# A feed-forward pair whose product banks ScalarE fills beforehand, with another order of products and of weight sums

## The chip, the core and the metric

The kernel runs on one core of a Trainium2 chip. Its engines are TensorE (PE in the profile), VectorE (DVE), ScalarE (ACT), GpSimd (POOL) and SyncE (SP), which here issues the loads. The metric is the device time in us of one execution; for the kernel before it is the median of three runs.

## What is computed

Two batches, 512 and 256 tokens, go through the same trunk of two layers. The kernel treats them as T = 768 tokens in two halves of H = 384. A layer is a feed-forward, a token mixer (a gated recurrence in the first layer, windowed attention in the second) and a second feed-forward, each on a normalized input and added to x. The change lies in the four feed-forwards:

```
def swiglu_ffn(x, w1, w2):
    gate, up = jnp.split(x @ w1, 2, axis=-1)
    return (jax.nn.silu(gate) * up) @ w2
...
    x = x + 0.5 * swiglu_ffn(rmsnorm(x, norm_g[li, 0]), ffn_w1[li, 0], ffn_w2[li, 0])
```

The model width is 1024 and the hidden width 2816, which is 22 column blocks of 128.

## The kernel before, in words

**Numbers as pairs.** Every fp32 operand of a matmul is split in a high part (a cast on ScalarE: L208 for weights, L319 for data) and a low part (a subtraction on VectorE: L209, L320). A product step is three matmuls: high by high, high by low, low by high.

**A pair by seven products.** A pair (up_pair) computes for one column block the gate and the up half for both token halves. That is a 2x2 block product, and it is done with seven products p1 to p7 instead of eight, from sums of weight blocks and sums of data blocks. Each product is 12 matmuls of 128x384 on L513 (four blocks of the inner width, three matmuls each). The seven results are joined with additions; one line of the join keeps two products in one bank of PSUM, since TensorE can go on adding into a bank. Before, the order of products (table UP) is p1, p7, p2, p5, p4, p6, p3, and the banks are a (p1 and p2), c (p7 and p4), d (p5 and p3) and b (p6 alone). The join: ScalarE copies a (L530) and c (L533) out between their two products, VectorE does L539 (after p5), L543, L544, L547 and L545 (after p6), L550 and L552 (after p3), and ScalarE the two silu operations (L536 in the bank, L551). The result t of the first token half is given out after p6, that of the second, w, after p3.

**A group.** A feed-forward has 22 blocks. The first two are computed plainly (up_plain), blocks 2 to 19 as pairs in five groups of four blocks (the first group has the two plain blocks and two pairs), and the last two blocks as pairs once more; 20 pairs per feed-forward, 80 in all. Four results (two blocks, two halves) are gathered in mix: four subtractions (L422, L423, L433, L434) form the sums t1 to t4 that the second product needs, each split by a cast L319 and a subtraction L320. After four blocks follows down_quad, which multiplies the group with its rows of the second weight, again in seven products p1, p2, p5, p4, p7, p6, p3, now of 18 matmuls of 128x512 (L577, three token blocks), and adds each to x on VectorE (L599). Data factors: p1 takes b00, p2 b10, p3 b11, p4 t4, p5 t1, p6 t2, p7 t3.

**Weights.** They are staged ahead: raw blocks a11, a12, a21, a22 are loaded by SP's queue (L160 and L194, four raw buffers), two sums are formed by accumulating transfers on GpSimd's queue (into, L147: s3 += a11 for p7, a22 += a21 for p4), and two on VectorE in place (L215: the "second" sum a11 += a21 for p6, behind p5's split; the "fourth" sum a12 += a11 for p3, behind p4's split). Eight buffers hold split weights (WBUFS); a pair's product takes one, so staging runs seven products ahead: when a product ends and its buffer is free, the cast for the product after the next six starts. The low part of p5 is formed on GpSimd (L209 with engine POOL), that of the other six on VectorE.

**What sets the order.** The code is written in one order and a scheduler spreads it; each engine then runs its own list in order. PSUM has eight banks of 512 columns (ps). A reader of a bank must be done before the next product that uses the bank.

## Time and profile before

| what | value |
|---|---|
| median of three runs | 2768.75 us (2768.64 to 2768.89) |
| span of the profiled execution (first to last instruction) | 2767.2 us |
| TensorE busy | 2745.0 us, 99% |
| VectorE busy | 2206.5 us, 80% |
| ScalarE busy | 1386.0 us, 50% |
| GpSimd busy | 453.0 us, 16% |
| granted TensorE clock, mean | 0.999 |

The profile shows one execution. Its span leaves out what lies around the first and the last instruction, so the time of a run is some 1.5 us longer than a span. Times are in us unless marked ns. A row of the timeline has the start, the length, the engine, the line, the operation and its tiles, how many instructions are put together, and in brackets how long the engine stood idle ahead of it and what ended that. Names of tiles there: w are split weights, wr and s raw weights, tA data of 384 columns, big the split data, ps a bank of PSUM, x the residual.

### The profile page before, as it was taken

What the parts mean: (1) busy time and instruction counts of PE and PEld (TensorE: products, weight loads), DVE (VectorE), ACT (ScalarE), POOL (GpSimd) and SP (SyncE); (2) the same over time, 40 slices, a digit from 0 to 9 for tenths busy, and PEclk for the clock granted to TensorE, in tenths of its full rate; (3) what the DMA queues carried; (4) which work ended last, traced back from release to release, by engine and by line L of the source; (5) the groups of instructions that cost most, each with busy time, mean ns of one, the idle gap of its engine ahead of it and who ended that gap; (6) DMA issues with size and microseconds to landing.
All of it is one profiled execution on the core that took longest, in us unless ns stands there. A gap on an engine that the chain in (4) does not pass through costs nothing.

```text
span 2767.2 us, 40933 instructions
## 1 busy us (share of the span) xinstructions
PE 2745.0 (99%) x15117; PEld 2554.8 (92%) x15117; DVE 2206.5 (80%) x3766; ACT 1386.0 (50%) x2589; POOL 453.0 (16%) x491
## 2 busy tenths in 40 slices
PE   8999999999999999999999999999999999999998
PEld 8999999989999889999999999999888889999998
DVE  8788788767887888788878887887847868788877
ACT  7344444634455675444445543444458855444443
POOL 2111121200000101211111121111105611211111
PEclk9999999999999999999999999999999999999999
DMA  6554554851122743655444355544424422655443
GB/s 172 130 125 114 126 140 124 227 161 39 39 62 66 205 119 78 143 134 131 115 117 121 78 145 134 126 119 118 130 73 111 89 69 73 145 134 130 114 118 107
DMA packets 352040, 325.22 MB, mean 118 GB/s; under 512 B 14216, under 2 KB 271200, under 8 KB 351840
## 3 DMA queue, kind: packets, MB, share of 16 engines
q1 hardware_dynamic: 303040, 224.56, 27.7%
q0 software_dynamic: 44496, 84.56, 17.4%
q10 hardware_dynamic: 4304, 13.49, 1.3%
q8 instruction: 118, 1.93, 0.3%
q14 instruction: 82, 0.67, 0.1%
HBM read 225.82 MB, written 15.73 MB: 87 GB/s over the span
## 4 chain that ended last, share of the span: by engine, by line
PE 96%; DVE 2%; ACT 1%; DMA 1%; issue 0%; DVEq 0%; POOL 0%; SPq 0%; ACTq 0%; POOLq 0%
PE ps L513 42%; PE ps L577 21%; PE ps L315 6%; PE ps L316 6%; PE ps L314 6%; PE ps L760 5%; PE ps L823 3%; PE ps L928 1%; PE ps L1414 1%; PE ps L904 1%; PE ps L385 1%; PE ps L1426 0%; PE ps L1376 0%; PE ps L1427 0%; PE ps L1377 0%; PE ps L1181 0%
## 5 line engine op out<-in xcount | busy, mean ns | idle before, releaser
L513 PE MATMUL ps<-big,w 128*128 128x384 f32 x6720 | 1169.3, 334 | 0.0
L513 PEld LDWEIGHTS ps<-big,w 128*128 128x128 f32 x6720 | 1165.9, 188 | 1.7 <-ACT tA L530 0.2
L208 ACT CAST w<-wr 128x512 fp32r<-128x512 f32 x600 | 415.8, 707 | 689.2 <-PE ps L513 274.9
L577 PE MATMUL ps<-w,big 128*128 128x512 f32 x2520 | 575.7, 390 | 0.0
L577 PEld LDWEIGHTS ps<-w,big 128*128 128x128 f32 x2520 | 472.7, 188 | 98.0 <-ACT big L319 0.4
L209 DVE TENSOR_TENSOR w<-wr,w 128x512 fp32r<-128x512 f32 (+1 forms) x520 | 438.0, 846 | 145.9 <-ACT w L208 123.9
L147 POOL DMA_DIRECT2D s<-wr x126 | 109.8, 878 | 1250.3 <-DMA s<-in_ffn_w_dram 432.0
L599 DVE SCALAR_TENSOR_TENSOR x<-ps,x 128x512 f32<-128x512 f32 x468 | 302.4, 686 | 10.1 <-PE ps L316 10.0
L314 PE MATMUL ps<-big,w 128*128 128x384 f32 x640 | 219.6, 345 | 1.2 <-ACT w L175 0.9
L315 PE MATMUL ps<-big,w 128*128 128x384 f32 x640 | 215.7, 337 | 0.7 <-DVE big L320 0.7
L316 PE MATMUL ps<-big,w 128*128 128x384 f32 x640 | 214.6, 335 | 0.0
L319 ACT CAST big<-tA 128x384 fp32r<-128x384 f32 x296 | 148.0, 513 | 115.4 <-DVE tA L545 37.0
L147 POOL DMA_DIRECT2D wr<-wr x109 | 94.9, 871 | 518.3 <-DMA wr<-in_ffn_w_dram 165.9
L760 PE MATMUL ps<-w,big 128*128 128x512 f32 x756 | 177.1, 392 | 0.1
L320 DVE TENSOR_TENSOR big<-tA,big 128x384 fp32r<-128x384 f32 x296 | 168.0, 578 | 6.7 <-ACT big L319 4.7
L209 POOL TENSOR_TENSOR w<-wr,w 128x512 fp32r<-128x512 f32 x80 | 137.4, 1718 | 197.8 <-ACT w L208 195.8
L760 PEld LDWEIGHTS ps<-w,big 128*128 128x128 f32 x756 | 140.6, 188 | 29.1 <-DVE w L320 0.6
L215 DVE TENSOR_TENSOR wr<-wr,wr 128x512 f32<-128x512 f32 (+1 forms) x120 | 123.3, 1027 | 25.9 <-issue 23.6
L314 PE MATMUL ps<-w,big 128*128 128x512 f32 x336 | 134.6, 401 | 0.1
L316 PE MATMUL ps<-w,big 128*128 128x512 f32 x336 | 131.8, 392 | 0.5 <-DVE big L400 0.5
L315 PE MATMUL ps<-w,big 128*128 128x512 f32 x336 | 131.8, 392 | 0.0
L315 PEld LDWEIGHTS ps<-big,w 128*128 128x128 f32 x640 | 120.6, 188 | 2.0 <-DVE big L320 1.7
(214 smaller groups left out, 3504.0 us busy)
## 6 DMA issues: line engine op xcount, KB each, us to landing
wr<-in_ffn_w_dram SPq DMA_DIRECT2D x264, 512.0 KB, 4.0
s<-wr POOLq DMA_DIRECT2D x126, 256.0 KB, 4.8
s<-in_ffn_w_dram SPq DMA_DIRECT2D x120, 256.0 KB, 3.2
wr<-wr POOLq DMA_DIRECT2D x80, 256.0 KB, 3.8
wr<-in_hg_w_in_dram SPq DMA_DIRECT2D x32, 512.0 KB, 3.9
wr<-wr POOLq DMA_DIRECT2D x29, 512.0 KB, 4.6
spill<-x ACTq DMA_DIRECT2D x12, 512.0 KB, 4.0
kept<-big POOLq DMA_DIRECT2D x8, 768.0 KB, 9.7
```

The source lines that it names most:

```text
L147: self.nc.gpsimd.dma_start(out, src, accum_op=ALU.add)
L208: nc.scalar.copy(h, src)
L209: (eng or nc.vector).tensor_sub(l, src, h.bitcast(F32))
L314: nc.tensor.matmul(out, a[0], b[0], start=first, stop=False)
L315: nc.tensor.matmul(out, a[0], b[1], start=False, stop=False)
L316: nc.tensor.matmul(out, a[1], b[0], start=False, stop=last)
L319: self.nc.scalar.copy(hi, src)
L320: self.nc.vector.tensor_sub(lo, src, hi.bitcast(F32))
L513: self.nc.tensor.matmul(ps, a[x], b[y], start=first and k == 0 and i == 0, stop=k == 3 and i == 2, skip_group_check=True,)
L577: nc.tensor.matmul(ps, a[x], w[y], start=name == chain and kp == 0 and q == 0, stop=kp == 1 and q == 2, skip_group_check=True,)
L599: self.nc.vector.scalar_tensor_tensor(x, ps, c, x, ALU.mult, ALU.add)
L760: nc.tensor.matmul(ps, x[:, sl], y, start=fresh and k == 0 and q == 0, stop=k == 3 and q == 2, skip_group_check=True,)
```

## The change

The order of products becomes p1, p5, p6, p2, p7, p3, p4. Banks a (p1, p2) and d (p5, p3) are started by a product as before; banks b and c are filled by ScalarE first. After p1, L549 writes the negative of a into b, and p6 is added into b by TensorE; after p6, L555 copies b into c, and p7 and later p4 are added into c. L556 copies b out as well (v), L552 copies d (w), and L559 writes the silu to SBUF. VectorE keeps L562 (after p7), L565, L567 (after p3) and L571 (after p4). The second half's result is now given out first, after p3, and the first half's after p4, so ffn collects results by index. The first pair of a feed-forward takes for b and c the two banks that the last plain block had.

In the weights of pairs the second sum is formed in a21 (a21 += a11, behind p5's split) and the fourth takes it from there (a12 += a21, behind p2's split); p6 uses a21. GpSimd forms the low part of p4 instead of that of p5. The accumulation a22 += a21 is issued ahead of that into s3. At the end of a feed-forward, where the last two blocks are multiplied with the rest of the second weight, the token blocks 0 to 2 (the first half) now take the first of the two column blocks all three in a row before the second one is begun.

```
-UP = ("p1", "p7", "p2", "p5", "p4", "p6", "p3")
+UP = ("p1", "p5", "p6", "p2", "p7", "p3", "p4")
...
+    def seeded(self):
+        return self.wide.pop(0) if self.wide else self.ps(H)
...
         s3 = []
+        if up:
+            self.into(a21, a22)
         for i, src in enumerate(three):
...
-        self.into(a21, a22)
+        if not up:
+            self.into(a21, a22)
...
-        own = {"p1": [a11], "p2": [a12], "p3": [a12], "p4": [a22], "p5": [a21], "p6": [a11], "p7": s3}
+        own = {"p1": [a11], "p2": [a12], "p3": [a12], "p4": [a22], "p5": [a21], "p6": [a21 if up else a11], "p7": s3}
...
+                "second": lambda: nc.vector.tensor_add(a21, a21, a11),
+                "fourth": lambda: nc.vector.tensor_add(a12, a12, a21),
...
-        behind = {"p5": "second", "p4": "fourth"} if up else {}
+        behind = {"p5": "second", "p2": "fourth"} if up else {}
...
-            split(name, own[name], nc.gpsimd if up and name == "p5" else None)
+            split(name, own[name], nc.gpsimd if up and name == "p4" else None)
...
-        a, b, c, d = (self.ps(H) for _ in range(4))
-        v, w, t = (self.tmp(H) for _ in range(3))
+        a, d = (self.ps(H) for _ in range(2))
+        b, c = (self.seeded() for _ in range(2))
+        t, v, w = (self.tmp(H) for _ in range(3))
         p = lambda name, ps, first, last: self.product(key, name, FACTOR[name], ps, first, last)
         p("p1", a, True, False)
-        nc.scalar.copy(v, a)
+        nc.scalar.activation(b, a, AF.Copy, scale=-1.0)
         self.ahead()
-        p("p7", c, True, False)
-        nc.scalar.copy(w, c)
+        p("p5", d, True, False)
+        nc.scalar.copy(w, d)
+        self.ahead()
+        p("p6", b, False, True)
+        nc.scalar.copy(c, b)
+        nc.scalar.copy(v, b)
         self.ahead()
         p("p2", a, False, True)
-        nc.scalar.activation(a, a, AF.Silu)
+        nc.scalar.activation(t, a, AF.Silu)
         self.ahead()
-        p("p5", d, True, False)
-        nc.vector.tensor_sub(w, w, d)
+        p("p7", c, False, False)
+        nc.vector.tensor_sub(w, c, w)
+        self.ahead()
+        p("p3", d, False, True)
+        nc.vector.tensor_sub(v, d, v)
+        self.last_act = nc.scalar.activation(v, v, AF.Silu).ins
+        nc.vector.tensor_mul(w, v, w)
+        yield 1, w
         self.ahead()
         p("p4", c, False, True)
-        p("p6", b, True, True)
-        nc.vector.tensor_sub(v, v, b)
-        nc.vector.tensor_sub(t, c, v)
-        nc.vector.tensor_mul(t, t, a)
-        yield t
-        nc.vector.tensor_sub(w, w, v)
-        self.ahead()
-        p("p3", d, False, True)
-        nc.vector.tensor_add(v, v, d)
-        self.last_act = nc.scalar.activation(v, v, AF.Silu).ins
-        self.last_dve = nc.vector.tensor_mul(w, v, w).ins
-        yield w
+        self.last_dve = nc.vector.tensor_mul(t, c, t).ins
+        yield 0, t
...
-            for i, k in (((0, 0), (1, 0), (0, 1)), ((1, 1),))[b] if b < 2 else ((b, 0), (b, 1)):
+            for i, k in (((0, 0), (1, 0), (2, 0), (0, 1)), ((1, 1),), ((2, 1),))[b] if b < 3 else ((b, 0), (b, 1)):
```

Lines move: the weight cast is L215 in the changed kernel, its split L216, the sums L224 and L225, the data's cast and split L335 and L336, mix has L438, L439, L449 and L450, the products L531, those of the down quad L596, their addition L618, the accumulating transfer L151. Numbers behind a tile's name tell tiles of one kind apart.

ScalarE's list in the third pair of a group (first feed-forward, fourth group of blocks), from the silu of the pair ahead on; big are the split sums of the gather, wr and s3 raw weights. Before:

```order
L551 ACTIVATE tA_409_2798<-tA_409_2798 128x384
L530 COPY tA_429_2945<-ps_425_2941 128x384
L208 CAST w_432_2961<-s3_403_2772 128x512
L319 CAST big_419_2919<-tA_410_2799 128x384
L533 COPY tA_430_2946<-ps_427_2943 128x384
L208 CAST w_433_2977<-wr_401_2768 128x512
L319 CAST big_421_2927<-tA_392_2663 128x384
L536 ACTIVATE ps_425_2941<-ps_425_2941 128x384
L208 CAST w_434_2993<-wr_402_2770 128x512
L319 CAST big_422_2932<-tA_411_2800 128x384
L319 CAST big_423_2935<-tA_410_2799 128x384
L319 CAST big_424_2938<-tA_393_2664 128x384
```

After, with the new pair's banks ps_423 (a), ps_425 (b), ps_424 (d) and ps_426 (c):

```order
L335 CAST big_417_2905<-tA_407_2785 128x384
L549 ACTIVATE ps_425_2929<-ps_423_2927 128x384
L215 CAST w_430_2947<-wr_399_2756 128x512
L335 CAST big_419_2913<-tA_391_2652 128x384
L552 COPY tA_429_2933<-ps_424_2928 128x384
L335 CAST big_420_2918<-tA_407_2785 128x384
L335 CAST big_421_2921<-tA_409_2787 128x384
L335 CAST big_422_2924<-tA_389_2650 128x384
L215 CAST w_431_2964<-wr_399_2756 128x512
L555 COPY ps_426_2930<-ps_425_2929 128x384
L556 COPY tA_428_2932<-ps_425_2929 128x384
```

The copies of the new pair's second bank, L533 before, stood third from the top of the casts; L555, the copy that fills bank c, now stands behind three casts L335 of the gather and a weight cast.

VectorE's list at the same place, the gather itself (wr are the raw weights in which a sum is formed, tA the pair's results). Before:

```order
L552 TENSOR_TENSOR tA_410_2799<-tA_409_2798,tA_410_2799 128x384
L209 TENSOR_TENSOR w_432_2961<-s3_403_2772,w_432_2961 128x512
L320 TENSOR_TENSOR big_419_2919<-tA_410_2799,big_419_2919 128x384
L422 TENSOR_TENSOR tA_410_2799<-tA_392_2663,tA_410_2799 128x384
L423 TENSOR_TENSOR tA_392_2663<-tA_393_2664,tA_392_2663 128x384
L209 TENSOR_TENSOR w_433_2977<-wr_401_2768,w_433_2977 128x512
L433 TENSOR_TENSOR tA_393_2664<-tA_393_2664,tA_410_2799 128x384
L320 TENSOR_TENSOR big_421_2927<-tA_392_2663,big_421_2927 128x384
L434 TENSOR_TENSOR tA_411_2800<-tA_411_2800,tA_393_2664 128x384
L215 TENSOR_TENSOR wr_401_2768<-wr_401_2768,wr_402_2770 128x512
```

After:

```order
L567 TENSOR_TENSOR tA_409_2787<-tA_408_2786,tA_409_2787 128x384
L571 TENSOR_TENSOR tA_407_2785<-ps_406_2784,tA_407_2785 128x384
L336 TENSOR_TENSOR big_415_2886<-tA_409_2787,big_415_2886 128x384
L216 TENSOR_TENSOR w_418_2908<-wr_398_2754,w_418_2908 128x512
L336 TENSOR_TENSOR big_417_2905<-tA_407_2785,big_417_2905 128x384
L438 TENSOR_TENSOR tA_409_2787<-tA_391_2652,tA_409_2787 128x384
L439 TENSOR_TENSOR tA_391_2652<-tA_389_2650,tA_391_2652 128x384
L216 TENSOR_TENSOR w_430_2947<-wr_399_2756,w_430_2947 128x512
L449 TENSOR_TENSOR tA_389_2650<-tA_389_2650,tA_409_2787 128x384
L336 TENSOR_TENSOR big_419_2913<-tA_391_2652,big_419_2913 128x384
L450 TENSOR_TENSOR tA_407_2785<-tA_407_2785,tA_389_2650 128x384
L224 TENSOR_TENSOR wr_399_2756<-wr_399_2756,wr_398_2754 128x512
```

Before, the chain to the last subtraction L434 began with L552; now it begins with L571, has L567 ahead of it and one more split L336 within, and ends with L450; the sum of raw weights stands behind it in both.

TensorE's list in the down quad of the same group: p2 (factor b10, tile big_416 before, big_417 after) and p5 (factor t1, big_421 before, big_419 after), with the banks of the three token blocks. Before:

```order
L577 MATMUL ps_465_3230<-w_453_3130,big_416_2894 128x512
L577 MATMUL ps_465_3230<-w_454_3131,big_416_2894 128x512
...
L577 MATMUL ps_466_3238<-w_453_3130,big_416_2894 128x512
...
L577 MATMUL ps_467_3246<-w_453_3130,big_416_2894 128x512
...
L577 MATMUL ps_472_3286<-w_455_3177,big_421_2927 128x512
L577 MATMUL ps_472_3286<-w_456_3178,big_421_2927 128x512
```

After:

```order
L596 MATMUL ps_463_3214<-w_451_3116,big_417_2905 128x512
L596 MATMUL ps_463_3214<-w_452_3117,big_417_2905 128x512
...
L596 MATMUL ps_470_3270<-w_453_3146,big_419_2913 128x512
L596 MATMUL ps_470_3270<-w_454_3147,big_419_2913 128x512
...
L596 MATMUL ps_471_3278<-w_453_3146,big_419_2913 128x512
L596 MATMUL ps_471_3278<-w_454_3147,big_419_2913 128x512
L596 MATMUL ps_471_3278<-w_453_3146,big_419_2913 128x512
L596 MATMUL ps_464_3222<-w_451_3116,big_417_2905 128x512
...
L596 MATMUL ps_465_3230<-w_451_3116,big_417_2905 128x512
```

Before, p5 followed all three token blocks of p2; now its first token block and half of its second stand ahead of p2's second.

22 lines of the change are left out of this document (16 added, 6 removed).

## The prediction

> **What bounds the kernel now.** I read the page first: busy time, and the chain that ended last by engine.
>
> ```profile
> span 2767.2 us, 40933 instructions
> PE 2745.0 (99%) x15117; PEld 2554.8 (92%) x15117; DVE 2206.5 (80%) x3766; ACT 1386.0 (50%) x2589; POOL 453.0 (16%) x491
> PE 96%; DVE 2%; ACT 1%; DMA 1%; issue 0%; DVEq 0%; POOL 0%; SPq 0%; ACTq 0%; POOLq 0%
> ```
>
> TensorE is busy for 99% of the span and carries 96% of the chain. The change touches what stands around the products of the pairs (L513) and of the down quads (L577) and takes no matmul away. So the next view is that of line L513 alone: how long TensorE stood before these matmuls, and who waited for them.
>
> ```profile
> L513 PE MATMUL ps<-big,w x6720: 333/334/445, 52.1 to 2742.7; 128*128 128x384 f32 x198
> its engine sat idle before it (us, times) until:
>   ACT tA L530: 0.2, 1
> who waited for it (us, times):
> ...
>   ACT tA L533: 82.9, 76
>   DVE tA L539: 78.6, 59
> ```
>
> In 6720 matmuls TensorE waited once. The readers of the banks wait for TensorE instead: ScalarE's L533 in 76 of 80 pairs, VectorE's L539 in 59. The 21 that are missing there are pairs in which VectorE came late and TensorE still did not wait. The timeline gives the pace, and the chain in order of time the price of that one wait (start, us, what).
>
> ```profile
> 299.80 42.28 PE L513 MATMUL ps<-big,w 128*128 128x384 f32 x243
> 341.92 28.76 PE L577 MATMUL ps<-w,big 128*128 128x512 f32 x126
> 52.23 29.25 PE ps L513 x168
> 457.55 29.14 PE ps L513 x168
> ```
>
> A matmul of 128x384 takes 0.1733 us (243 in 42.28, the last one's 0.33 overlapping), so a product of 12 takes 2.08 and a pair of 84 takes 14.56; one of 128x512 takes 28.76/126 = 0.227 (nearly). Two pairs take 29.14 where nothing waits and took 29.25 at the start of the first feed-forward: that is the wait, 0.11 us. The kernel ends when TensorE has done its work, so an operation taken from VectorE or ScalarE is worth nothing by itself. The question is whether the new order makes TensorE wait.
>
> **The change, part by part.** *The join.* New operations are named by the changed kernel's lines. Per group of instructions the columns are busy us, mean ns | idle before.
>
> ```profile
> L544 DVE TENSOR_TENSOR tA<-ps,tA 128x384 f32<-128x384 f32 x80 | 44.2, 552 | 0.8
> L536 ACT ACTIVATE ps<-ps 128x384 f32<-128x384 f32 x80 | 38.0, 475 | 57.8 <-PE ps L513 57.8
> ```
>
> VectorE had seven operations of this size per pair, of 0.55 us each, and keeps four: 3 x 80 x 0.55 = 132 us less. ScalarE goes from four to six: 2 x 80 x 0.475 = 76 us more, each costed as L536, which reads and writes a bank as the new L549 and L555 do. VectorE is at 80% and ScalarE at 50%, neither carries the chain, so both sums are worth 0 while their work stays ahead of TensorE. TensorE's own work is the same 84 matmuls; a product that adds into a filled bank issues the same matmuls as one that starts a bank, so 0.
>
> What is new is three short links, each with one product of cover: p1, then L549 on ScalarE, then p6; p6, then L555, then p7; p7, then L562 on VectorE, then p4. In an ordinary pair the cover holds. Let S be the start of a pair; the pair below starts at S = 341.92 - 2 x 14.56 = 312.80.
>
> ```profile
> 313.62 0.55 DVE L550 TENSOR_TENSOR tA<-tA,ps 128x384 f32<-128x384 f32 x1
> 314.08 0.69 DVE L209 TENSOR_TENSOR w<-wr,w 128x512 fp32r<-128x512 f32 x1
> 315.08 0.48 ACT L530 COPY tA<-ps 128x384 f32<-128x384 f32 x1 [0.35 <-PE ps L513]
> 315.16 0.56 DVE L552 TENSOR_TENSOR tA<-tA,tA 128x384 f32<-128x384 f32 x1
> 315.45 0.62 ACT L208 CAST w<-s 128x512 fp32r<-128x512 f32 x1
> 315.97 0.52 ACT L319 CAST big<-tA 128x384 fp32r<-128x384 f32 x1
> 316.11 0.69 DVE L209 TENSOR_TENSOR w<-s,w 128x512 fp32r<-128x512 f32 x1 [0.40 <-ACT w L208]
> 319.62 0.62 ACT L208 CAST w<-wr 128x512 fp32r<-128x512 f32 x1
> 319.91 0.55 DVE L434 TENSOR_TENSOR tA<-tA,tA 128x384 f32<-128x384 f32 x1
> 320.49 1.34 ACT L319 CAST big<-tA 128x384 fp32r<-128x384 f32 x3 [0.25 <-DVE tA L434]
> 321.74 0.62 ACT L208 CAST w<-wr 128x512 fp32r<-128x512 f32 x1
> 324.21 0.54 DVE L539 TENSOR_TENSOR tA<-tA,ps 128x384 f32<-128x384 f32 x1
> ```
>
> The copy of the first product starts at 315.08, 0.20 after that product's end at S + 2.08, and takes 0.48. What comes from ScalarE to TensorE takes 0.15 more: at the start of the first feed-forward a copy L530 delayed p2 by the 0.11 found above,
>
> ```profile
> 52.07 6.19 PE L513 MATMUL ps<-big,w 128*128 128x384 f32 x34
> 55.72 0.47 ACT L530 COPY tA<-ps 128x384 f32<-128x384 f32 x1
> ```
>
> and p2 was due at 52.07 + 4.16 = 56.23, so it started at 56.34, 0.15 after that copy's end at 56.19. A link so takes 0.20 + 0.48 + 0.15 = 0.83 of the 2.08 that the product between gives: 1.25 us are spare in each ordinary pair, and the same for L562 with 0.55 instead of 0.48. Cost 0. If the cover were gone, each us of queue beyond 1.25 would be a us of the kernel.
>
> *The pair after a gather.* There the queue is long, and this is where the sum is made. Four groups of each of four feed-forwards have such a pair (the third of the group), and the first pairs of the second to fourth feed-forward follow the gather of the plain columns: 16 + 3 = 19. In the new order ScalarE has the casts of the last three sums of the gather (t4, t3, t2) and one weight cast ahead of L555, and these wait for VectorE's chain that ends in L450 (L434 before). Before, the copy L533 stood ahead of them.
>
> The chain starts earlier now. Its first operation is the last multiply, L571, which can start at S + 0.20, where L552 started at 315.16 = S + 2.36. But L567, ahead of it, can be held by GpSimd's split of p4, which the change puts here. Its cast starts 0.20 after p3's end (S - 2.08), thus at S - 1.88, and ends at S - 1.26.
>
> ```profile
> 305.06 0.61 ACT L208 CAST w<-wr 128x512 fp32r<-128x512 f32 x1
> 305.76 1.29 POOL L209 TENSOR_TENSOR w<-wr,w 128x512 fp32r<-128x512 f32 x1 [1.97 <-ACT w L208]
> 320.13 0.87 POOL L147 DMA_DIRECT2D s<-wr  x1 [6.39 <-DVE big L320]
> 320.38 2.50 DVE L215 TENSOR_TENSOR wr<-wr,wr 128x512 f32<-128x512 f32 x1
> 320.69 1.63 POOL L209 TENSOR_TENSOR w<-wr,w 128x512 fp32r<-128x512 f32 x1
> ```
>
> GpSimd starts 0.09 after its cast (305.06 + 0.61 to 305.76) and takes 1.29 alone: S - 1.17 to S + 0.12. A VectorE operation with both inputs in SBUF that met such a split, L215 at 320.38, ended at 322.88, 0.56 after GpSimd's 322.32 instead of 0.68 after its own start; scaled to L567's 0.55 that is 0.45, so L567 ends at S + 0.57 and L571 starts 0.09 before that (operations start that much before the end shown of the one ahead, 313.62 + 0.55 = 314.17 against the next at 314.08), at S + 0.48. The Trainium skill, page "SBUF — State Buffer", section "Who interferes with whom", says that whichever of the two starts first holds the shared access for its whole instruction and blocks the other fully. By that rule L567 would run whole after GpSimd, 0.10 later than I take; in this case's trace the operation needed less than its own time after GpSimd's end, so the measurement decides.
>
> From the chain's first operation to its last took 320.46 - 315.16 = 5.30 before. The new chain has one more split of a hidden block in it (+0.46, as from 313.62 to 314.08) and loses the idle 0.40 that stood before 316.11: 5.36. L450 ends at S + 5.84. Then 0.03 to the casts (320.46 to 320.49), 1.25 for the three (to 321.74), 0.52 for the weight cast (315.45 to 315.97), 0.48 for L555 and 0.15 to TensorE: S + 8.27. p7 is due after four products, at S + 8.32. So the sum stands 0.05 us inside; with no hold by GpSimd it would stand 0.33 inside. With so little spare, some pairs will fall on the other side of the line, and I take 0.05 us of wait a pair on average: 19 x 0.05 = 0.95 us. Ends: 0 (no better, since there is no wait here to save), and the 0.65 a pair of the first rival.
>
> VectorE's link in that pair: L539 was held to 324.21 by the same backlog, S + 11.41. L562 inherits that place at the worst; with 0.55 and 0.15 it is done at S + 12.11, due for p4 at S + 12.48. Cost 0.
>
> *The down quad.* There the order now starts p5 after 24 matmuls instead of 36.
>
> ```profile
> 342.59 1.22 DVE L209 TENSOR_TENSOR w<-wr,w 128x1024 fp32r<-128x1024 f32 x1
> 344.19 0.55 DVE L552 TENSOR_TENSOR tA<-tA,tA 128x384 f32<-128x384 f32 x1
> 344.66 0.69 DVE L599 SCALAR_TENSOR_TENSOR x<-ps,x 128x512 f32<-128x512 f32 x1
> 348.87 0.56 DVE L320 TENSOR_TENSOR big<-tA,big 128x384 fp32r<-128x384 f32 x1
> ```
>
> Let D = 341.92 be its start. p5's sixth matmul needs the low half of t1, by D + 29 x 0.227 - 0.15 = D + 6.43. Before, that split came 4.68 after L552. Between the same two there are now two accumulations fewer (2 x 0.69), one split more (0.46) and one of 128x1024 (1.22): 4.98. From L571 at D + 0.20 to 0.48 and with its own 0.56 it ends at D + 5.7 to 6.0, at least 0.4 early. Cost 0; if VectorE comes 0.6 later than that, 0.2 a quad, 4 us in 20.
>
> *The weights.* Casts, splits and sums are the same in number; p4's split takes p5's place on GpSimd. The second sum must now follow p5's split and p6's cast follows that sum: they are on the path to L555 only in the gather pair, where the sum is done before the three casts are. Of the accumulating transfers on GpSimd's queue (320.13 is one) none is added. SP's loads of the feed-forwards keep their order. What is staged is 7 products, 14.5 us, ahead, so a split that lands 1 us later costs 0. At the end of a feed-forward the first half's values now come last. They are needed after three adds of six matmuls, 18 x 0.227 = 4.09 after p4; L571 (0.55), w's split (0.56), t's cast (0.52) and split (0.56) behind the 0.20 make 2.39: 0.
>
> *Sum.* The one wait of 0.11 goes, since in the first pair L555 stands ahead of the casts. 0.95 - 0.11 = 0.84 on the profiled span of 2767.2 gives 2768.0; 1.55 lies around that span in the median run (2768.75), so **2769.6 us**. A measurement of this kernel can tell about 0.2%, 5.5 us, from no change.
>
> **The rivals.** *GpSimd in the way, slower.* The split of p4 often does not run alone. At 320.69 it started 0.36 later than its cast allowed (319.62 + 0.62 + 0.09 = 320.33), behind the issue of a transfer at 320.13, and took 1.63. With the longer time alone L567 ends 0.34 later and L555 is 0.29 too late: 19 x 0.29 = 5.5, 2774.3. With the issue ahead too, 0.65 too late: 12.4, 2781.1. With one half of the pairs of each kind, 2777.7. It decides where L450 ends later than S + 5.89. For it: of the two splits quoted one is of the long kind. Against it: at S - 1.9 VectorE has just got its operand from TensorE and meets GpSimd with one such operation, not with a row of them as at 320.38.
>
> *The down quad waits.* t1's low half comes late by 0.2: 2769.6 + 4 = 2773.6. For it: a backlog such as that at 324.21. Against it: 0.4 to 0.7 spare.
>
> *Relief pays, faster.* VectorE loses 132 us, and TensorE's wait for it at the start of a feed-forward (us, times, longest) shrinks.
>
> ```profile
> PE ps L315 <- DVE big L320: 0.7, 2, 0.3
> ```
>
> With the 0.1 above that is at most 0.8: 2767.9. To be faster by over 0.2% it would have to find 5.5 us, which no wait on these lines holds.
>
> **How the numbers follow.** Forecast, 0 to 0.2 us of wait a pair (2768.6 to 2772.5): 0.62. GpSimd in the way: 0.24, of which 0.17 lies above 2774.25. The down quad: 0.07, of which 0.01 above. Relief: 0.07, of which I leave 0.03 for a gain that the waits do not show. So faster 0.03, same 0.79, slower 0.18. The range goes from 2767.0 (relief, less the 0.25 us between the runs of before and as much again for waits too short for the views, and rounded down) to 2778.0, which leaves out 0.10 at the slower rival's upper end and some 0.04 at the other side.
>
> **What would show it.** Right: the products' line again without waits, or with a few of under 0.3 us, all on ScalarE's L555 and in the third pair of a group; VectorE's busy time near 2075, ScalarE's near 1462; L450 ending near S + 5.85. The slower rival: GpSimd's split of p4 at 1.6 us or more and L567 ending behind it in the pair before, with 0.3 to 0.7 us of wait on L555 each time. Wrong altogether: waits of TensorE on L549 or L562 in ordinary pairs, a pace other than 0.173 us for products into filled banks, or a time under 2763.

## The result, and the profile after

| what | before | after |
|---|---|---|
| median of the runs on one chip | 2768.69 us (2768.46 to 2768.89, four runs) | 2807.51 us (2802.03 to 2809.55, four runs) |
| span of the profiled execution | 2767.2 us | 2807.8 us (that run: 2809.55 us) |

The ratio is 1.0137, with an interval of 1.0124 to 1.0151: the kernel became 1.4% slower. The forecast was 2769.6 us, with a range up to 2778.0. It was wrong, in size and in place. Of the executions of all the kernels below one stands apart, one of ten of weights_only with 3904.03 us; the ratio given there is of the other nine.

One statement ahead of the prediction must be corrected first. The accumulating transfer into(out, src) adds src to out, so into(a21, a22) makes **a21 += a22, the operand of p5**, and p4 uses the raw a22. The text says in two places that the transfer is a22 += a21 and makes the operand of p4. The change moves p5 from the fourth place to the second, so the product that comes early is the one whose operand arrives by a transfer.

The page of the changed kernel, busy time and the chain that ended last:

```profile
PE 2760.6 (98%) x15117; PEld 2550.0 (91%) x15117; DVE 2104.8 (75%) x3526; ACT 1440.3 (51%) x2749; POOL 443.8 (16%) x491
PE 70%; DVE 13%; DMA 9%; ACT 4%; issue 3%; POOL 1%; ACTq 0%; DVEq 0%; POOLq 0%; SPq 0%
```

VectorE lost 240 instructions (3766 to 3526) and ScalarE gained 160, as forecast, and VectorE is 102 us less busy (2105, forecast 2075; ScalarE 1440, forecast 1462). TensorE's share of the chain fell from 96% to 70%; VectorE, the transfers and ScalarE came in. The waits of TensorE (what it waited for: us, times, longest):

```profile
PE ps L596 <- DVE x L618: 14.5, 17, 3.1
...
PE ps L531 <- DVE tA L562: 5.5, 4, 1.9
...
PE ps L531 <- ACT ps L555: 0.5, 3, 0.2
```

L596 are the matmuls of the down quads. Before, VectorE's additions to x (L599 then, L618 now) held them once, for 0.3 us. The view of waits has 17 such waits; the distances between the starts of neighbouring matmuls, which also hold what follows a wait, show the short ones too. Counted is what exceeds the usual distance (0.226 us in quads, 0.173 in pairs) by more than 0.06:

| part | before | after | where in a quad of 126 matmuls |
|---|---|---|---|
| quads, up to the 100th matmul | 0.3 us | 15.4 us (14 of 20 quads over 0.2) | from the 19th on, p2's first, into p1's first bank |
| quads, from the 100th on | 0.0 us | 10.0 us (17 of 20) | from the 109th on, p3's first, into p7's first bank |
| pairs | 0.1 us | 7.9 us | 6.6 of it at p4 behind L562, in the pair after each fifth quad; 1.3 at p7 behind L555, in the first pair of the later three feed-forwards |

These make 32.9 of the 40.6 us between the two spans. The other 7.7 lie in smaller distances and outside pairs and quads, and were not followed. The new order of token blocks at a feed-forward's end was not tried alone; edges_old below has it too and is 5.8 us slower in all.

**The 109th matmul.** A bank of p7 is free for p3 when VectorE has added it to x. In the quad that starts at D = 348.00 the chain in order of time runs through VectorE's list from one sum of the second weight (L229) to that addition:

```profile
359.59 1.14 DVE wr L229
...
360.75 4.37 DMA wr<-in_ffn_w_dram
...
365.78 5.82 DMA wr<-wr
...
371.75 0.63 ACT w L215
...
372.41 0.69 DVE w L216
373.10 0.61 DVE x L618
...
373.85 4.33 PE ps L596 x18
```

A raw weight block of the coming pair is loaded (4.37 us) when the sum has freed its buffer, then a22 is added into a21 by a transfer from SBUF to SBUF (issued at 365.78, 5.82 us), then ScalarE casts p5's high part and VectorE forms the low part. Only behind that step stands the addition that frees the bank. VectorE's own rows there, with the idle time in brackets:

```profile
367.77 0.68 DVE L216 TENSOR_TENSOR w<-wr,w 128x512 fp32r<-128x512 f32 x1
372.41 0.69 DVE L216 TENSOR_TENSOR w<-wr,w 128x512 fp32r<-128x512 f32 x1 [3.96 <-ACT w L215]
373.02 0.69 DVE L618 SCALAR_TENSOR_TENSOR x<-ps,x 128x512 f32<-128x512 f32 x1
```

VectorE is idle for 3.96 us, waiting for a weight that TensorE needs only a product (2.08 us) after the quad's end, and the additions of p7 wait behind it in its list. Nothing else holds them: VectorE has been idle since 368.45. TensorE started 1.44 after the step L216; the matmul was due at D + 108 x 0.2266 = D + 24.47, so VectorE must go on, that is start the step it waited for, by D + 23.03. It went on at D + 24.41 here, at D + 23.88 in the median of the 20 quads. The same place before, in the quad that starts at 341.92:

```profile
361.63 0.88 POOL L147 DMA_DIRECT2D wr<-wr  x1 [6.05 <-DVE w L209]
...
363.28 1.88 DVE L599 SCALAR_TENSOR_TENSOR x<-ps,x 128x512 f32<-128x512 f32 x3
...
365.07 0.69 DVE L209 TENSOR_TENSOR w<-wr,w 128x512 fp32r<-128x512 f32 x1
367.90 0.69 DVE L215 TENSOR_TENSOR wr<-wr,wr 128x512 f32<-128x512 f32 x1 [2.14 <-issue]
```

The transfer was issued later, 19.71 us after the quad's start against 17.78 now. VectorE had its idle time here too (2.14 us, and the row names no releaser) and went on at D + 25.98, later than now. But the three additions at 363.28 stood ahead of it, not behind it: p5 was the fourth product, so its steps stood further down the list. So it held nobody.

**The 19th matmul.** The worst case is the first quad of the kernel, D = 80.33:

```profile
79.94 2.00 ACT L215 CAST w<-wr 128x1024 fp32r<-128x1024 f32 x2 [5.10 <-DMA wr<-wr]
81.02 1.23 DVE L216 TENSOR_TENSOR w<-wr,w 128x1024 fp32r<-128x1024 f32 x1 [4.09 <-ACT w L215]
82.16 0.55 DVE L565 TENSOR_TENSOR tA<-ps,tA 128x384 f32<-128x384 f32 x1
...
83.78 0.55 DVE L571 TENSOR_TENSOR tA<-ps,tA 128x384 f32<-128x384 f32 x1
...
86.99 0.69 DVE L618 SCALAR_TENSOR_TENSOR x<-ps,x 128x512 f32<-128x512 f32 x1
```

and TensorE there:

```profile
80.33 4.28 PE L596 MATMUL ps<-w,big 128*128 128x512 f32 x18
87.73 4.44 PE L596 MATMUL ps<-w,big 128*128 128x512 f32 x12 [3.12 <-DVE x L618]
```

Here the late weight is the quad's own p5. ScalarE waits 5.10 us for its accumulating transfer, VectorE 4.09 us for the cast. In VectorE's list this split of 1.23 us stands ahead of the last pair's join (L565, L567, L571), which opens the gather, which stands ahead of the first L618. That one starts at D + 6.66; before it started 2.74 after D in the quad of the prediction's rows (344.66 less 341.92), and it must start by D + 18 x 0.2266 - 0.74 = D + 3.34. The median over the 20 quads went from 2.74 to 3.66. Why the quad's p5 comes later: the last raw block that its transfer needs goes into the buffer that the last pair's a22 leaves, and a22 is now held by p4, the last product, whose low part GpSimd forms. In the fourth quad (D = 348.00):

```profile
333.88 1.63 POOL L216 TENSOR_TENSOR w<-wr,w 128x512 fp32r<-128x512 f32 x1
...
339.75 0.88 POOL L151 DMA_DIRECT2D wr<-wr  x1 [4.25 <-DMA wr<-in_ffn_w_dram]
...
344.37 1.05 ACT L215 CAST w<-wr 128x1024 fp32r<-128x1024 f32 x1 [1.86 <-DMA wr<-wr]
345.45 1.22 DVE L216 TENSOR_TENSOR w<-wr,w 128x1024 fp32r<-128x1024 f32 x1 [0.85 <-ACT w L215]
```

In the median the load of that block starts at D - 12.48, 0.03 after GpSimd's split ends, against D - 14.39 before; the accumulation is issued at D - 8.07 against D - 9.74, and VectorE splits the quad's p5 at D - 2.31 against D - 3.91. It takes both the place and the engine: p5_second below, where GpSimd forms p4's low part but p4 is the fifth product, loses nothing at the 19th, and join_only, where p4 is last but VectorE splits it, 2.6 us.

**The pair after the fifth quad.** L562 frees the way for p4, and VectorE comes late to it, behind six updates of x (L611 and L612) and the weights' steps:

```profile
1493.13 0.68 DVE L611 TENSOR_TENSOR x<-x 128x512 f32<-128x512 f32 x1
...
1501.43 0.55 DVE L562 TENSOR_TENSOR tA<-ps,tA 128x384 f32<-128x384 f32 x1
```

TensorE stands for 1.93 us ahead of p4. It happens once in each of the four feed-forwards, for 0.82 to 1.93 us each.

**The place of the forecast's sum**, the third pair of a group. At S = 318.88:

```profile
324.78 1.34 ACT L335 CAST big<-tA 128x384 fp32r<-128x384 f32 x3 [1.11 <-DVE tA L450]
...
326.55 0.47 ACT L555 COPY ps<-ps 128x384 f32<-128x384 f32 x1
```

The casts start at S + 5.90 (forecast S + 5.87), L555 at S + 7.67 and is done at S + 8.14, 8.12 by the forecast. The step that leads there came as forecast too: GpSimd's split of p4 runs from S - 1.17 to S + 0.11, and L567, held by it, ends at S + 0.52 (forecast S + 0.57). No third pair waits. The one sum that was worked out to the hundredth came out, and it was not where the time went.

### The profile page after: what moved, and what is told of

Read it like the earlier page. It is cut to its first block, busy times and chain, and to the rows that moved or that the text cites. A ratio compares the mean times of both kernels' runs of the same rounds, so it can differ in the third digit from the quotient of the medians.

```text
span 2807.8 us, 40688 instructions
## 1 busy us (share of the span) xinstructions
PE 2760.6 (98%) x15117; PEld 2550.0 (91%) x15117; DVE 2104.8 (75%) x3526; ACT 1440.3 (51%) x2749; POOL 443.8 (16%) x491
## 4 chain that ended last, share of the span: by engine, by line
PE 70%; DVE 13%; DMA 9%; ACT 4%; issue 3%; POOL 1%; ACTq 0%; DVEq 0%; POOLq 0%; SPq 0%
PE ps L531 29%; PE ps L596 12%; PE ps L331 6%; PE ps L332 6%; PE ps L330 6%; PE ps L779 4%; DMA wr<-wr 4%; DVE w L216 3%; PE ps L842 3%; DMA wr<-in_ffn_w_dram 3%; DVE x L618 2%; DVE big L336 2%; ACT w L215 2%; PE ps L947 1%; PE ps L1433 1%
## 5 line engine op out<-in xcount | busy, mean ns | idle before, releaser
L531 PE MATMUL ps<-big,w 128*128 128x384 f32 x6720 | 1171.7, 334 | 6.0 <-DVE tA L562 5.5
L531 PEld LDWEIGHTS ps<-big,w 128*128 128x128 f32 x6720 | 1165.0, 188 | 11.1 <-DVE tA L562 6.8
L215 ACT CAST w<-wr 128x512 fp32r<-128x512 f32 x600 | 414.2, 706 | 617.0 <-PE ps L531 165.6
L216 DVE TENSOR_TENSOR w<-wr,w 128x512 fp32r<-128x512 f32 (+1 forms) x520 | 427.4, 829 | 250.8 <-ACT w L215 240.2
L596 PE MATMUL ps<-w,big 128*128 128x512 f32 x2520 | 587.3, 392 | 15.1 <-DVE x L618 14.5
L596 PEld LDWEIGHTS ps<-w,big 128*128 128x128 f32 x2520 | 470.0, 188 | 127.4 <-DVE x L618 17.1
L618 DVE SCALAR_TENSOR_TENSOR x<-ps,x 128x512 f32<-128x512 f32 x468 | 306.4, 684 | 14.7 <-PE ps L332 13.7
L151 POOL DMA_DIRECT2D s<-wr x126 | 110.7, 886 | 1222.2 <-DVE wr L229 350.2
L335 ACT CAST big<-tA 128x384 fp32r<-128x384 f32 x296 | 146.8, 512 | 133.0 <-DVE tA L438 44.5
L216 POOL TENSOR_TENSOR w<-wr,w 128x512 fp32r<-128x512 f32 x80 | 124.6, 1558 | 397.1 <-ACT w L215 397.1
L336 DVE TENSOR_TENSOR big<-tA,big 128x384 fp32r<-128x384 f32 x296 | 164.1, 566 | 25.8 <-ACT big L335 21.4
L779 PE MATMUL ps<-w,big 128*128 128x512 f32 x756 | 177.2, 392 | 0.1
L151 POOL DMA_DIRECT2D wr<-wr x109 | 95.1, 873 | 403.3 <-DVE x L618 121.6
L330 PE MATMUL ps<-w,big 128*128 128x512 f32 x336 | 134.7, 401 | 1.3 <-ACT big L415 0.7
L331 PE MATMUL ps<-w,big 128*128 128x512 f32 x336 | 131.8, 392 | 0.0
L332 PE MATMUL ps<-w,big 128*128 128x512 f32 x336 | 131.7, 392 | 0.0
L331 PEld LDWEIGHTS ps<-big,w 128*128 128x128 f32 x640 | 120.4, 188 | 2.7 <-DVE big L336 2.6
L330 PEld LDWEIGHTS ps<-big,w 128*128 128x128 f32 x640 | 119.8, 188 | 3.2 <-ACT w L179 1.7
```

The source lines that it names most:

```text
L151: self.nc.gpsimd.dma_start(out, src, accum_op=ALU.add)
L215: nc.scalar.copy(h, src)
L216: (eng or nc.vector).tensor_sub(l, src, h.bitcast(F32))
L330: nc.tensor.matmul(out, a[0], b[0], start=first, stop=False)
L331: nc.tensor.matmul(out, a[0], b[1], start=False, stop=False)
L332: nc.tensor.matmul(out, a[1], b[0], start=False, stop=last)
```

## The experiments

All times are medians beside runs of the kernel before on the same chip. The three numbers in brackets are the excess of the distances between matmuls, as in the table above: quads up to the 100th matmul / from there on / pairs. The kernel before has 0.3 / 0.0 / 0.1, the changed one 15.4 / 10.0 / 7.9.

**Which pairs carry the loss?** Four kernels take the old order, join and sums for some pairs of each feed-forward and the new ones for the rest. With the list set to (4, 8, 12, 16, 20) it is the first pair after each quad (first_old), with (3, 7, 11, 15, 19) the last pair before each (last_old), with both lists edges_old, with (6, 10, 14, 18) the third pair of the groups (third_old).

```
-                self.plan_quad((tag, i), (gate, up), (NC, P), UP)
+                self.plan_quad((tag, i), (gate, up), (NC, P), UPO if i in PLAIN_PAIRS else UP)
...
+        if j in PLAIN_PAIRS:
+            yield from self.up_pair_old(tag, j)
+            return
```

> The first pair behind each down quad (blocks 4, 8, 12, 16, 20) keeps the order, join and weight sums of before; the other 60 pairs are changed. Theory, three places (in the trace of the changed kernel TensorE stands 15.4 us at the 19th matmul of the down quads, where p2 adds into p1's banks behind VectorE's late L618, 10.0 us at the 109th, where p3 adds into p7's banks while VectorE is blocked by the split of the next pair's p5, and 6.6 us on L562 in the pair after the fifth quad): the second and third place go, the first stays: 2807.5 - 16.6 = 2791, waits at the 109th matmul under 1 us in all, at the 19th still about 15. Rival, the new join costs the same in every pair (38.8/80 = 0.49 us): 20 pairs give back 9.7, 2797.8. Forecast's own mechanism (ScalarE's chain in the pair after a gather): nothing, 2807.

Measured: 2792.29 us, ratio 1.0082 (1.0067 to 1.0097), (15.9 / 0.0 / 1.4). As expected: the 109th matmul no longer waits, and the waits in the pairs after the fifth quad are gone too.

> The last pair ahead of each down quad (blocks 3, 7, 11, 15, 19) keeps what was before, the other 60 are changed. Theory of the three places: its second result comes out after p3 and its first after p6 as before, so VectorE's gather is done earlier, L618 follows p1 in time and the 15.4 us at the 19th matmul go; the other two places stay: 2807.5 - 15.4 = 2792. Rival, the same cost in every pair: 2797.8. Forecast's own mechanism: 2807.

Measured: 2844.51 us, ratio 1.0272 (1.0255 to 1.0289), (0.6 / 58.4 / 9.5). The 19th is free, as expected, but the kernel is 37 us slower than the changed one. The waits of TensorE:

```profile
PE ps L635 <- DVE x L657: 41.8, 21, 3.7
```

Nearly all are at the 109th now (L657 is the addition to x here). VectorE goes on at D + 25.64 in the median, against 23.88, because the transfer comes later after D: it is issued at D + 19.24 in the median, against D + 17.97. It is issued at D + 19.2 to 19.5 in the kernels whose last pair ahead of a quad ends with p3 (the kernel before, this one, and edges_old, weights_only, p5_second and p5_second_pool below), and at D + 17.5 to 18.0 where that pair ends with p4; why was not followed. So taking away one place made the other worse, and the sizes of the two can't be added or taken away one by one. It is not that the wait at the 19th had hidden the other. In the changed kernel a longer wait at the 19th moves the transfer and VectorE back by about as much: in the first quad 4.8 us are lost there, VectorE goes on at D + 28.08, and the 109th loses 0.2.

> First and last pair of each group (both sets, 40 pairs) keep what was before. Theory of the three places: both savings add up, 2807.5 - 32 = 2775.5; what is left over 2768.7 is the start of the second to fourth feed-forward (L555, 1.3 us) and some 4 us outside the pairs and quads. Rival, the same cost in every pair: 2807.5 - 19.4 = 2788.

Measured: 2774.64 us, ratio 1.0019 (1.0010 to 1.0028), (0.9 / 0.0 / 1.3). As expected. Half of the pairs have the new join, order and sums, and that costs 5.8 us in all.

> The third pair of the later groups (blocks 6, 10, 14, 18, sixteen pairs: those that follow a gather) keeps what was before. Theory of the three places: these pairs carry no wait, so nothing changes, 2807 (2803 to 2810). Rival, the same cost in every pair: 2807.5 - 7.8 = 2799.7. The forecast's place (L555 behind the casts of the gather): if the loss came from there, it would go almost whole, 2769 to 2775.

Measured: 2808.07 us, ratio 1.0135 (1.0120 to 1.0150), (14.1 / 5.7 / 12.3). As expected: the time of the changed kernel, though the three places share the loss otherwise. The place on which the forecast spent its care carries nothing.

**Is it the transfer, and what else stands in the list?** The kernel a22_dve leaves the accumulating transfer out in pairs. A sum on VectorE takes its place, a22 += a21 behind p5's split, so p5 uses a21 alone and p4 uses a21 + a22; these are other sums than the reference's, and the kernel is read for its waits alone. first_add has the first product of the quad written ahead of the gather, and the gather issued behind the first L618. both_fixes is the two together, with a22_dve's sums.

```
-        if up:
-            self.into(a21, a22)
...
+            if up and name == "p5":
+                pin(nc.vector.tensor_add(a22, a22, a21))
```

```
-                gather(ts, kp)
-            self.down_quad(tag, g, hid)
...
+                    quad = self.down_quad(tag, g, hid)
+                    next(quad)
+                    with self.tc.issue_after(self.first_add):
+                        gather(ts, kp)
+                    for _ in quad:
+                        pass
```

> All pairs are changed, but the sum a22 += a21 is formed by VectorE (behind p5's split) and not by an accumulating transfer, so the cast of p5 waits for the load of the raw weights alone; VectorE gets 80 additions of 0.68 us more. Theory (VectorE is blocked near the end of a down quad by the split of the next pair's p5, whose cast waits for the accumulating transfer into the same raw tile, and the L618 behind it frees p7's banks for p3): the 10.0 us at the 109th matmul go, and the 6.6 us on L562 in the pair after the fifth quad for the most part, since that backlog comes from the same wait; the 15 us at the 19th stay: 2793 (2789 to 2798). Rival, the raw load itself or the mere place of the split ahead of L618 holds VectorE: the waits at the 109th stay, 2807 or more for the added work.

Measured: 2802.82 us, ratio 1.0125 (1.0109 to 1.0140), (24.5 / 0.0 / 4.5). Without the transfer in the coming pair the 109th does not wait, as expected. The 19th grew from 15.4 to 24.5, which was not, and the time lies above the range on record. In this kernel the quad's own p5 is split later still, at D - 1.56 in the median against D - 2.31; why was not followed.

> All pairs are changed; in a group's end p1 of the down quad is written ahead of the gather, and the gather's subtractions are issued behind the first L618. Theory: L618 starts at D + 2.75 as before the change (now a median of 3.66), the waits at the 19th matmul go (at most 3 us stay, in quads where the split ahead waits for a transfer), and TensorE reaches the 109th matmul earlier, in time for the same block of VectorE: as in the run with the old last pairs, whose waits at the 109th rose from 10 to 50 us, 2840 (2830 to 2846). Rival, the loss in that run came from the mixture of old and new pairs itself: 2792.

Measured: 2800.59 us, ratio 1.0118 (1.0103 to 1.0133), (7.6 / 9.9 / 6.8). Neither number came out. The first addition starts at D + 3.16 in the median, and half of the excess at the 19th stays: in those quads the last pair's join itself is late behind p5's split, and the additions wait for it whatever their place. The 109th did not grow as in last_old, with half of the excess at the 19th gone.

> Both edits together, all 80 pairs with the new join: a22 += a21 on VectorE and p1 of the quad ahead of the gather. Theory: neither wait is left, and what remains over 2768.7 is the start of three feed-forwards (1.3 us), some of L562 after the fifth quad and the 4 us outside pairs and quads: 2773 (2770 to 2778). Rival, each place costs by itself and the run with the first add moved stays bad for another reason: over 2790.

Measured: 2796.45 us, ratio 1.0106 (1.0090 to 1.0121), (17.4 / 0.0 / 4.2). Not as expected: the time is the rival's. The same is left at the 19th, L565 behind the quad's own p5, which is late here as in a22_dve (D - 1.64).

> The kernel before with the weight part of the change alone: a21 += a11 behind p5's split, p6 from a21, the fourth sum from a21 behind p4's split, p4's low part on GpSimd, the accumulation into a22 issued first; the order of products and the join are those of before. Theory: p5 is the fourth product there, three L599 stand ahead of its split on VectorE, and no wait of TensorE arises: 2769 (2768 to 2772). Rival, the sums in the other operand are what costs: 2790 to 2810.

The opposite cut: the kernel before, with the new sums and with p4's low part on GpSimd, and the old order and join.

```
+        su = (a21, a11) if up else (a11, a21)
...
-            split(name, own[name], nc.gpsimd if up and name == "p5" else None)
+            split(name, own[name], nc.gpsimd if up and name == "p4" else None)
```

Measured: 2769.85 us, ratio 1.0003 (0.9993 to 1.0013), (0.5 / 0.0 / 2.5). As expected: with p5 in the fourth place neither the sums nor the swap of engines costs anything that can be told.

> All 80 pairs with the new join and the new weight sums; only the sum a21 += a22, p5's operand, is formed by VectorE ahead of p5's cast, in pairs and down quads, instead of by an accumulating transfer on GpSimd's queue (100 additions, 79 us more for VectorE). Theory (all waits come from p5's operand landing late, since p5 now stands second in a pair and the down quad's raw blocks are loaded later: at the 109th matmul VectorE is blocked by the next pair's p5 with L618 behind it, at the 19th by the quad's own p5 ahead of L565 and L571): both waits and most of L562's after the fifth quad go, 2773 (2770 to 2779). Rival, VectorE's order at the quad's start (L618 behind the gather) costs by itself: the waits at the 19th stay, 2785 to 2792. Rival, the join costs in every pair: above 2800.

The changed kernel with a21 += a22 formed by VectorE ahead of p5's cast, in pairs and quads; the sums are the reference's, and no accumulating transfer into a21 is left.

```
-            self.into(a21, a22)
...
+            if name == "p5":
+                pin(nc.vector.tensor_add(a21, a21, a22))
```

Measured: 2793.23 us, ratio 1.0090 (1.0075 to 1.0105), (0.4 / 0.0 / 18.3). In the quads everything is gone: without the transfer neither wait is there. But the time is 20 us above the number on record, since another wait came, in all 16 third pairs:

```profile
PE ps L529 <- DVE tA L560: 13.1, 16, 0.8
```

L560 is L562 of the changed kernel. The forecast gave that link 0.37 us of spare there. The added sum of the coming pair (L235) stands ahead of it in VectorE's list, and VectorE then stands until the cast behind the sum is done:

```profile
323.38 0.68 DVE L235 TENSOR_TENSOR wr<-wr 128x512 f32<-128x512 f32 x1
324.80 0.69 DVE L212 TENSOR_TENSOR w<-wr,w 128x512 fp32r<-128x512 f32 x1 [0.73 <-ACT w L211]
```

**Which part of the change brings p5 to the front of the list?** p5_second is the kernel before with p5 second (order p1, p5, p7, p2, p4, p6, p3), the second sum behind p2, and p4's low part on GpSimd instead of p5's; p5_second_pool the same order with p5's low part left on GpSimd. join_only is the changed kernel with the old sums and with p5's low part on GpSimd, join_p4_pool the same with p4's on GpSimd: one word apart. p5_pool is the changed kernel, new sums too, with p5's on GpSimd.

```
-            split(name, own[name], nc.gpsimd if up and name == "p5" else None)
+            split(name, own[name], nc.gpsimd if up and name == "p4" else None)
```

> The kernel before, with the old join and the old sums, but with p5 moved from the fourth to the second place (p1, p5, p7, p2, p4, p6, p3) and its low part formed by VectorE, p4's by GpSimd; the second sum stays behind the fourth product. Theory: VectorE's list has the split of p5 ahead of the three additions of p7; its operand lands as late as before the change (VectorE went on at D + 25.5), TensorE needs p7's banks at D + 24.5 and gets them 1.44 after VectorE goes on: 2.4 us in each of 20 quads, 2768.7 + 48 = 2817 (2795 to 2825). Rival, the join with filled banks is what costs: 2769.

Measured: 2828.14 us, ratio 1.0212 (1.0197 to 1.0227), (0.0 / 59.2 / 0.4).

```profile
PE ps L577 <- DVE x L599: 40.6, 19, 3.5
```

Slower by 60 us with the old join, and above the range on record. It waits at the 109th alone, in all 20 quads.

> As the run with p5 moved to the second place in the kernel before (2828.1), but p5's low part stays on GpSimd. Order, join and sums are the same as there. Theory (not the place of p5 as such costs, but that a step of p5 that waits for its transfer stands in VectorE's list ahead of the additions that free p7's banks): the three additions stand ahead of everything that waits, 2770 (2768 to 2773). Rival, the earlier demand for p5's operand costs by itself, on whatever engine: 2800 or more.

Measured: 2775.22 us, ratio 1.0026 (1.0016 to 1.0037), (0.0 / 0.0 / 5.4). With p5's split on GpSimd the same order costs 6 us instead of 60, some 2 above the range on record; 4.6 us of its excess lie in the pairs after the fifth quads.

> The changed kernel, but GpSimd forms the low part of p5 as before the change, VectorE that of p4. Theory: the last raw block of a group is free some 0.7 us earlier (VectorE's 0.68 instead of GpSimd's 1.3 or more), the quad's own p5 lands earlier and the waits at the 19th matmul shrink from 15 to under 8; at the 109th the sum L224 now waits for GpSimd's split of p5 behind the landing (0.62 and 1.3 to 1.6 us instead of 0.66), with all three additions behind it: 10 grows to some 35. Together 2824 (2812 to 2832). Rival, the split of p5 on VectorE is itself the trouble, not its operand: the waits at the 109th go, 2790 to 2797.

Measured: 2839.43 us, ratio 1.0257 (1.0242 to 1.0272), (7.2 / 36.0 / 21.5). Worse than the changed kernel, as expected, and by more. With the new sums the second sum a21 += a11 overwrites p5's operand, so VectorE's list has a step that must follow GpSimd's split. Here is that step (L224), after the split:

```profile
377.14 0.62 ACT L215 CAST w<-wr 128x512 fp32r<-128x512 f32 x1 [4.31 <-DMA wr<-wr]
377.84 1.28 POOL L216 TENSOR_TENSOR w<-wr,w 128x512 fp32r<-128x512 f32 x1 [5.15 <-ACT w L215]
...
379.16 0.69 DVE L224 TENSOR_TENSOR wr<-wr,wr 128x512 f32<-128x512 f32 x1 [4.45 <-POOL w L216]
379.77 1.88 DVE L618 SCALAR_TENSOR_TENSOR x<-ps,x 128x512 f32<-128x512 f32 x3
```

4.45 us of VectorE's time are lost ahead of the same additions. New sums tie VectorE to p5 whichever engine splits it.

> The changed kernel's order and join with the weight sums of before: a11 += a21 behind p5's split, p6 from a11, p5's low part on GpSimd, a12 += a11 behind p2's split. Theory: the order, not the operand of the sums, makes the loss, so it is at least as slow as the changed kernel; the second sum must now also wait until s3 += a11 has read a11 (another transfer): 2824 (2807 to 2840). Rival, the loss comes from forming the second sum in the other operand: near 2770.

Measured: 2782.64 us, ratio 1.0054 (1.0037 to 1.0070), (2.6 / 0.0 / 7.5). Both numbers on record missed: it is neither near p5_pool nor without cost. The old second sum, a11 += a21, only reads p5's operand and need not wait for GpSimd's split. The rows at the quad's end, D = 342.98:

```profile
360.84 0.88 POOL L151 DMA_DIRECT2D wr<-wr  x1 [4.10 <-DVE x L615]
...
365.79 0.69 DVE L226 TENSOR_TENSOR wr<-wr,wr 128x512 f32<-128x512 f32 x1 [1.76 <-DMA wr<-wr]
366.40 1.28 DVE L615 SCALAR_TENSOR_TENSOR x<-ps,x 128x512 f32<-128x512 f32 x2
```

VectorE goes on with the sum when the transfer has landed, and two additions (L615) follow 0.61 later, at D + 23.42. They are the second and third of p7: the first stands ahead of the sum here, at 363.35, and that is the bank that the 109th matmul needs. TensorE started 0.83 after such an addition in the changed kernel (373.02 to 373.85), so even for the first bank D + 23.64 would have been in time.

> As the join with the weight sums of before (2782.6), but p5's low part is formed by VectorE and p4's by GpSimd, as the change has it. Theory: VectorE now has the split of p5 and the second sum ahead of all three additions of p7 and goes on with the first about 1.9 us later than at D + 22.7, where 0.3 are spare: 1.5 us in each of 20 quads; with GpSimd's longer split the group's last raw block is free later and some waits at the 19th matmul come back: 2816 (2803 to 2828). Rival, with the sums of before the join has no wait at the 109th wherever the split is made: 2780 to 2786.

Measured: 2809.72 us, ratio 1.0146 (1.0131 to 1.0161), (12.4 / 19.1 / 3.8). As expected. The same place, D = 348.91:

```profile
366.72 0.88 POOL L151 DMA_DIRECT2D wr<-wr  x1 [3.56 <-DVE x L615]
...
372.34 0.62 ACT L212 CAST w<-wr 128x512 fp32r<-128x512 f32 x1 [4.56 <-DMA wr<-wr]
372.99 0.69 DVE L213 TENSOR_TENSOR w<-wr,w 128x512 fp32r<-128x512 f32 x1 [3.32 <-ACT w L212]
373.60 0.68 DVE L226 TENSOR_TENSOR wr<-wr,wr 128x512 f32<-128x512 f32 x1
374.20 1.88 DVE L615 SCALAR_TENSOR_TENSOR x<-ps,x 128x512 f32<-128x512 f32 x3
```

The transfer is issued at D + 17.81, against D + 17.86 in join_only. Then the cast, the split and the sum stand ahead of the additions: 1.86 us from the cast's start to the first L615, where join_only has 0.61 from the sum's, and the transfer itself took 5.62 to the cast's start, against some 4.9. The additions start at D + 25.29, TensorE waits. And at the quad's start the second effect, the quad's own p5, in join_only and in join_p4_pool:

```profile
333.37 0.86 POOL L151 DMA_DIRECT2D wr<-wr  x1 [3.36 <-DMA wr<-in_ffn_w_dram]
...
339.49 1.22 DVE L213 TENSOR_TENSOR w<-wr,w 128x1024 fp32r<-128x1024 f32 x1
```

```profile
334.88 1.63 POOL L213 TENSOR_TENSOR w<-wr,w 128x512 fp32r<-128x512 f32 x1
...
340.96 0.88 POOL L151 DMA_DIRECT2D wr<-wr  x1 [4.45 <-DMA wr<-in_ffn_w_dram]
...
346.66 1.23 DVE L213 TENSOR_TENSOR w<-wr,w 128x1024 fp32r<-128x1024 f32 x1 [1.16 <-ACT w L212]
```

GpSimd's split of p4, at the group's end, holds the raw block: the accumulation is issued at D - 7.95 instead of D - 9.61 and the split starts at D - 2.25 instead of D - 3.49. One word, which of two products' low parts GpSimd forms, is worth some 26 us (40.7 over the kernel before, against 14.3), and brings the old sums to the time of the whole change.

**The place in the list, over all kernels.** Counted in each of the 20 quads, all three additions of p7 stand behind the step that waits for the transfer in each kernel that loses time at the 109th (the changed one, last_old, third_old, first_add, p5_second, p5_pool, join_p4_pool). In join_only two stand behind it, and in the kernel before, weights_only and p5_second_pool none, and these four lose nothing there.

No kernel here beats the kernel before.

## Why the prediction was wrong, point by point

- **The bound, right.** TensorE set the end, the change took none of its work away, and 102 us less of VectorE's time gave nothing.
- **The join, right.** Ordinary pairs don't wait on L549, L555 or L562, and products into filled banks keep their pace. edges_old, with half of the pairs in the new form, stays within 5.8 us.
- **The pair after a gather, right** to 0.03 us where it was worked out; the forecast 0.95 us is 0 in these 16 pairs and 1.3 in the three first ones. GpSimd held L567 much as the forecast had it, so the step is right and not only its number; but the margin was thin. The rival "GpSimd in the way" decided at L450 later than S + 5.89, and L450 ended at S + 5.87. The rivals' times there start from 2768.75 and leave out the 0.11 that the sum takes off; nothing hangs on that. third_old shows that the place carries nothing.
- **"The weights", wrong, and this is the step that failed.** It said "a split that lands 1 us later costs 0". That holds for TensorE, which needs the weight later. It does not hold for VectorE, which waits for it in the order of its list. The direction of into was misread, so that the transfer was thought to serve a product that comes late; and of the moved product only its own time was costed, not what is queued behind it. The runs put there: p5 second with its split on VectorE, 60 us alone (p5_second), 6 with the split on GpSimd (p5_second_pool), 1 (not clear of the noise) with the old order and the same swap of engines (weights_only).
- **"The down quad. Cost 0", wrong.** It followed t1's low half to p5, with 0.4 us to spare. It did not follow L618, which frees p1's bank for p2 (15.4 us) and p7's for p3 (10.0 us). The rival "The down quad waits" names the right part and the wrong link, and its price, 4 us, is a sixth of the measured one.
- **"VectorE's link in that pair. Cost 0", right for the third pair, wrong for the pair after the fifth quad**, which was not looked at: 6.6 us in all.
- **The chances.** Of the 0.18 for slower 0.17 came from GpSimd in the way, which did not happen, and 0.01 from the down quad, where the time was lost.

The cause, as the runs bear it out, is a product of two parts of the change. The new order puts p5 second; the swap of engines puts p5's low part in VectorE's list (and, with the new sums, p5's sum is bound to it too). Together they put a step that waits for an accumulating transfer ahead of the additions that free PSUM banks. Taking away the transfer (a21_dve) clears both places in the quads, and moving the split away with the old sums (join_only, p5_second_pool) clears the 109th. At the 19th the swap acts the other way round as well: GpSimd's split of p4, the last product now, delays the load that the quad's own p5 needs (join_only against join_p4_pool).

What stays open: why VectorE goes on anywhere between D + 22.8 (join_only) and D + 25.9 (weights_only), so that sizes at the 109th were forecast badly (the transfer is issued at D + 17.6 in the one and D + 19.4 in the other, which is 1.8 of these 3.1 us); what the last 7.7 us of the span are; and the 3.8 us of join_only outside its counted waits. That the loads of the weights slow the transfer down is one possibility, and it was not tried.

## What to carry to other kernels

When an order changes on an engine that runs its list in order, look for each step that waits for a transfer and ask what stands behind it in the list, above all work that frees a bank or buffer; the time when the step's own result is needed says nothing on that. An operand that arrives by a transfer belongs late in the list, or on an engine that nobody waits for. Taking away one such wait can make another worse (last_old), so repair them together and measure the sum.

## What the runs showed of the hardware

After a long stand TensorE does not come back at full pace. In the first quad it stood 3.12 us, to 87.73. What follows, as two windows (length, busy time of PE, PEld, DVE, ACT and POOL, then the granted clock, the DMA share and GB/s):

```profile
87.70:90.60 2.90, 2.87 (x7) 2.29 (x8) 2.90 (x7) 2.40 (x5) 0.00 (x0) 0.50 0.52 153
91.00:95.00 4.00, 4.00 (x20) 3.29 (x19) 3.64 (x7) 0.00 (x0) 0.00 (x0) 1.00 0.21 58
```

The granted clock is 0.50 for about 3 us, with matmuls 0.43 apart instead of 0.226, and then 1.00 again: some 1.6 us more, lost behind a stand of 3.1. Over all runs, counted in pairs and quads by the idle time in brackets, none of 144 stands of 0.5 to 1.85 us was followed by it; of 12 from there to 2.0 us five were, of 23 from 2.0 to 2.9 us 17, and of 8 longer ones six, all but one of 2.97 (p5_second) and one of 3.18 (last_old). The usual loss was 1.5 to 1.7 us. So a wait of 3 us at a place that repeats 20 times can cost half as much again, and that is most of why last_old and p5_second have 58 and 59 us of excess where the waits add up to 41.8 and 40.6. The Trainium skill, page "TensorE: Matmul & The Clock Gate", section "Why this matters for your kernels", advises no idle gaps of TensorE over about 3 us, since one window of idle time takes the clock back to half. The half clock agrees with these runs; the limit does not quite, since stands of 1.85 to 2.9 us already had it at times.

An accumulating transfer of 256 KB within SBUF took 5.82 us from issue to landing (365.78 above) and 4.97 in the next quad; in join_only 4.92 to the start of the cast behind it. The Trainium skill, page "DMA: Bandwidth & Descriptors", section "Anatomy of one DMA — SWDGE (gpsimd) path", gives 2.0 us plus the bytes by 436 KB per us for a transfer that GpSimd issues, 2.6 us here by an estimate from it; these runs show about twice that.

VectorE and GpSimd hold each other up where both work on operands in SBUF. L567 of the changed kernel takes 0.56 us in the pair at 332.71 and 1.30 us in the third pair at 318.10, where GpSimd's split of p4 runs from 317.71 to 318.99. It ends 0.41 us after that split, which is less than its own time; all 16 third pairs show the same.
